# Residual blocks as whole rows: one DMA of 128x1024 in place of two of 128x512, and a new table of engine orders, in a two-layer hybrid decoder

## The chip, the core and the metric

The kernel runs on one core of a Trainium2 chip. The metric is the device time of one execution in microseconds (us), taken as the median of several. The core has a matmul engine (PE, with its weight loads PEld), a vector engine (DVE), an activation engine (ACT), GpSimd (POOL), and SyncE (SP), which issues every DMA of this kernel in one queue, in order.

## What is computed

Two decoder layers over x of 1024 tokens by 1024 features, all in float32. Cut to what matters here:

```python
for l in range(DEPTH):                      # 2
    proj = rmsnorm(x, attn_norm[l]) @ w_in[l]
    ... # four mixers: latent attention, gated convolution, pooling, sliding-window attention
    mixed = group_norm(stack(y_a, y_b, y_c, y_d)) * mix_norm[l]
    x = x + mixed @ w_o[l]                  # the residual add of this change
    gate, up = split(rmsnorm(x, ffn_norm[l]) @ w_gate_up[l])
    x = x + (silu(gate) * up) @ w_down[l]
return rmsnorm(x, final_norm)
```

## The kernel before, in words

Everything is kept transposed: a block is 128 features by 1024 tokens, there are 8 blocks d, and a block has two halves t of 512 tokens. Float32 products are made of three matmuls (`mm3`, L294) on numbers split in two parts: ACT rounds (`CAST`, L305 for data, L237 for weights), DVE subtracts (L306, L238). So every operand that PE reads has passed ACT and then DVE.

On-chip memory for blocks is a pool of 47 slots of 128x1024 (`Slots`), given out first in, first out while the program is written; a slot serves as a pair (128x1024) or as two halves. A DMA into a slot waits until the last reader of what was there before is done.

The stage of this change is the latent attention of a layer, steps n = 0 to 7, each one head and one half of the queries: scores (L1223 to L1225), softmax on DVE and ACT (L1231 to L1261), then, one step later, `mix_values`: PE transposes the probabilities (L1277), ACT and DVE split them (L305, L306), PE multiplies them with the values (L1289, into `ps_pv`), and L1304 and L1305 take the result away. Between these steps `out_some` issues the output projection in 16 pieces (`out_part`, d = 0 to 7, t = 1 then 0), each 18 matmuls into `ps_mm` with the groups b, c, d of `mixed`; group a is added later in `out_last`. L1327 adds a piece to its half of the residual x. That half comes from memory by `fetch_x` (L1343). The first three blocks (`NSP`) go back to memory as "mixed blocks" (`xp`, L1329) and are read again in `out_last` (L1397). The weights of a piece (`w_o`, L228) are loaded and split one block ahead. At the end of the stage the weights `w_oa` (L281) and the first weights of the feed-forward part (`w_gu`, L1435) follow.

The order in which each engine runs its instructions is not that of the program. `order_engines` collects the instructions in steps, gives each a place (its rank in the program plus an entry of the table `MOVES` for its group), and `arrange` walks through them with a table of durations: when an engine is free, it takes the ready step with the lowest place. The result is written out as a fixed order per engine, SP's DMA queue too. So both a new slot assignment and a new `MOVES` change the order on all engines, in stretches that the edited lines don't touch as well.

Of the kernel before, what the change touches and what calls it, by code (L numbers as in the profile page):

```python
# [22 lines left out]
HT = 512  # L23
NK = D // P
# [10 lines left out]
HALVES = (1, 0)  # L35
OUT_PARTS = tuple((d, t) for d in range(NK) for t in HALVES)
# [7 lines left out]
NSP = 3  # L44
# [78 lines left out]
def trunk_kernel(ctx: ExitStack, tc: tile.TileContext, ins, out):  # L123
    nc = tc.nc
    act, dve, pe, pool, sp = nc.scalar, nc.vector, nc.tensor, nc.gpsimd, nc.sync
# [254 lines left out]
    x_in = ins["xT"]  # L380
# [195 lines left out]
    for l in range(L):  # L576
# [735 lines left out]
        def out_part(d, t):  # L1312
            if t == HALVES[0]:
                out_w[:] = take()
                ahead()
            w = out_w
            s = residual.pop(0)
            if len(parts):
                fetch_x()
            p = ps("mm")  # L1320
            terms = []
            for k in (4, 5, 2, 3, 0, 1):
                hl = mixed["bcd"[k // 2], k % 2, t]
                ks = slice(k * P, (k + 1) * P)
                terms.append((w[0][:, ks], w[1][:, ks], R.ap(hl[0]), R.ap(hl[1])))
            mm3(p, terms)
            dve.tensor_tensor(out=F.ap(s), in0=F.ap(s), in1=p, op=ALU.add)  # L1327
            if d < NSP:
                sp.dma_start(xp[d][:, t * HT : (t + 1) * HT], F.ap(s))  # L1329
                F.free(s)  # L1330
            else:
                x[d][t] = s

        parts = deque(OUT_PARTS)
        coming = deque(OUT_PARTS)
        residual, out_w = [], []

        def fetch_x():
            if coming:
                d, t = coming.popleft()  # L1340
                s = F.half()
                src = x_in[d] if l == 0 else xs[d]
                sp.dma_start(F.ap(s), src[:, t * HT : (t + 1) * HT])  # L1343
                residual.append(s)
# [145 lines left out]
        for n, (h, t) in enumerate(steps):  # L1490
# [8 lines left out]
            if n == 0:  # L1499
# [13 lines left out]
                fetch_x()  # L1513
# [625 lines left out]
def arrange(steps, rank=lambda v: v.rank):  # L2139
# [380 lines left out]
```

## Time and profile before

| | |
|---|---|
| median of 3 runs | 2036.31 us (2035.26 to 2036.7) |
| the profiled execution | 2037.59 us, span of its instructions 2035.7 us |
| PE, PEld, DVE, ACT, POOL busy | 99%, 82%, 81%, 50%, 10% |
| DMA | 320.21 MB, q1 (SP's) 45.9% of 16 engines' span |
| residual loads L1343 | 32 of 256 KB, mixed blocks out L1329 12 and back L1397 12, of 256 KB |

PE is busy almost all the time, and busy time of PE is not a measure of what could be won, since its matmuls overlap. What can be won or lost is in the stretches where PE stands still, and these are found by the idle time in front of its instructions. The span has two such stretches by nature: the start, until the first blocks are loaded and split, and the end, where the last normalization and stores follow the last matmul. A row of a timeline gives start and duration, the engine, the line, and in brackets the idle time before it with what ended it.

### The profile page before, as it was taken

How to read it: one execution, taken by the hardware profiler on the slowest of the kernel's cores; microseconds unless marked ns; L12 is line 12 of the kernel's file. 1: busy time of each engine (PE TensorE's matmuls, PEld its weight loads, DVE VectorE, ACT ScalarE, POOL GpSimd, SP SyncE). 2: the span in 40 equal slices, each digit the busy share in tenths (PEclk: the TensorE clock that was granted, in tenths of full speed). 3: DMA queues.
4: the chain of work that ended last, by engine and by line, in shares of the span. 5: the costliest groups of instructions: out<-in, count | busy, mean ns of one | idle time of the engine just before them, and what ended most of it. 6: DMA issues, size and time to landing. Idle time of an engine off the chain costs nothing.

```text
span 2035.7 us, 26489 instructions
## 1 busy us (share of the span) xinstructions
PE 2015.7 (99%) x9378; PEld 1669.5 (82%) x9378; DVE 1646.4 (81%) x2793; ACT 1027.6 (50%) x1803; POOL 212.7 (10%) x212
## 2 busy tenths in 40 slices
PE   9999999999999999999999999999999999999998
PEld 8887888778888888888888878887888888888887
DVE  8889988998888888755778998989977787886555
ACT  7447666653333435433545676668433233355342
POOL 0000000013213213000000000000232212220000
PEclk9999999999999999999999999999999999999999
DMA  5101222346566667875455113241554454497652
GB/s 184 55 27 36 75 95 99 126 141 220 210 221 223 217 231 256 305 243 176 147 176 168 38 37 98 73 139 66 195 183 150 150 184 146 152 323 264 200 173 90
DMA packets 166949, 320.21 MB, mean 157 GB/s; under 512 B 13600, under 2 KB 85408, under 8 KB 166816
## 3 DMA queue, kind: packets, MB, share of 16 engines
q1 hardware_dynamic: 166816, 318.51, 45.9%
q8 instruction: 74, 1.21, 0.2%
q14 instruction: 59, 0.48, 0.1%
HBM read 220.41 MB, written 98.04 MB: 156 GB/s over the span
## 4 chain that ended last, share of the span: by engine, by line
PE 90%; DVE 5%; ACT 2%; DMA 2%; issue 1%; SPq 0%; DVEq 0%; ACTq 0%
PE ps_mm L294 34%; PE ps_s L294 28%; PE ps_t L294 11%; PE ps_pv L294 8%; PE ps_pv L1289 2%; PE ps_t L1277 1%; PE ps_s L1223 1%; PE ps_s L1225 1%; PE ps_s L1224 1%; DVE u L306 1%; PE ps_mm L1109 1%; PE ps_pv L814 1%; PE ps_s L753 1%; PE ps_t L802 1%; DVE u L309 1%
## 5 line engine op out<-in xcount | busy, mean ns | idle before, releaser
L294 PE MATMUL ps_mm<-u,u 128*128 128x512 f32 (+1 forms) x3402 | 852.3, 388 | 1.8 <-ACT u L305 0.8
L294 PEld LDWEIGHTS ps_mm<-u,u 128*128 128x128 f32 x3402 | 623.9, 188 | 128.2 <-issue 2.9
L294 PE MATMUL ps_s<-u,u 128*128 128x512 f32 x2628 | 645.8, 389 | 0.0
L294 PEld LDWEIGHTS ps_s<-u,u 128*128 128x128 f32 x2628 | 492.6, 188 | 103.6 <-ACT tn L458 1.0
L306 DVE TENSOR_TENSOR u<-u,u 128x1024 fp32r<-128x1024 f32 (+2 forms) x400 | 413.1, 1050 | 170.1 <-ACT u L305 123.2
L305 ACT CAST u<-u 128x1024 fp32r<-128x1024 f32 (+2 forms) x400 | 343.3, 881 | 407.8 <-PE ps_s L294 88.6
L294 PE MATMUL ps_t<-u,u 128*128 128x512 f32 (+1 forms) x1142 | 283.6, 377 | 0.9 <-DVE u L1408 0.6
L172 POOL TENSOR_TENSOR u<-u 128x256 f32<-128x256 f32 x176 | 205.9, 1171 | 748.7 <-DMA u<-in_w_dn 395.2
L294 PEld LDWEIGHTS ps_t<-u,u 128*128 128x128 f32 x1142 | 209.1, 188 | 41.7 <-DVE u L1408 1.1
L294 PE MATMUL ps_pv<-u,u 128*128 128x512 f32 x696 | 175.6, 390 | 0.2 <-ACT tn L458 0.2
L294 PEld LDWEIGHTS ps_pv<-u,u 128*128 128x128 f32 x696 | 130.4, 188 | 27.9 <-ACT tn L458 0.6
L1605 ACT ACTIVATE tp<-tp 128x512 f32<-128x512 f32 x84 | 53.1, 632 | 124.2 <-DVE tp L372 124.2
L1286 POOL MEMSET u<- 128x128 f32 x32 | 6.5, 231 | 857.0 <-DVE sm L1255 404.9
L305 ACT CAST u<-ps_t 128x512 fp32r<-128x512 f32 (+4 forms) x136 | 64.6, 507 | 60.8 <-PE ps_t L1277 32.9
L308 ACT ACTIVATE u<-u,par 128x512 fp32r<-128x512 f32 x100 | 69.5, 717 | 44.6 <-DVE u L372 14.9
L306 DVE TENSOR_TENSOR u<-ps_t,u 128x512 fp32r<-128x512 f32 (+4 forms) x136 | 76.3, 584 | 13.9 <-ACT u L305 13.1
L309 DVE SCALAR_TENSOR_TENSOR u<-u,par,u 128x512 fp32r<-128x512 f32 x100 | 73.2, 749 | 7.2 <-ACT u L308 7.0
L1606 DVE TENSOR_TENSOR tp<-tp,u 128x512 f32<-128x512 f32 x84 | 62.7, 747 | 13.4 <-ACT tp L1605 12.6
L458 ACT COPY tn<-ps_s 128x512 f32<-128x512 f32 x66 | 38.5, 583 | 67.1 <-PE ps_s L294 67.0
L340 ACT ACTIVATE tn<-u 128x512 f32<-128x512 f32 (+1 forms) x92 | 51.9, 592 | 38.2 <-DVE u L1883 35.3
L372 DVE TENSOR_TENSOR tp<-tp,u 128x512 f32<-128x512 f32 x80 | 60.6, 757 | 1.2
L1289 PE MATMUL ps_pv<-u,u 128*128 128x512 f32 (+2 forms) x184 | 51.9, 356 | 2.3 <-ACT u L305 2.3
(222 smaller groups left out, 2172.9 us busy)
## 6 DMA issues: line engine op xcount, KB each, us to landing
u<-in_w_gu SPq DMA_DIRECT2D x88, 512.0 KB, 3.8
ad<-u SPq DMA_DIRECT2D x154, 256.0 KB, 3.1
u<-ad SPq DMA_DIRECT2D x70, 512.0 KB, 5.0
u<-in_w_dn SPq DMA_DIRECT2D x68, 512.0 KB, 4.8
qd<-u SPq DMA_DIRECT2D x44, 512.0 KB, 3.0
u<-qd SPq DMA_DIRECT2D x32, 512.0 KB, 4.7
u<-in_w_in SPq DMA_DIRECT2D x29, 512.0 KB, 3.5
u<-ws SPq DMA_DIRECT2D x28, 512.0 KB, 3.5
```

What stands on the lines that cost most here:

```text
L172: pool.tensor_tensor(out=o, in0=o, in1=u, op=ALU.add)
L294: pe.matmul(o, w, r, start=start and k == 0 and i == 0, stop=stop and k == n - 1 and i == 2, skip_group_check=again,)
L305: act.copy(hi, f)
L306: dve.tensor_tensor(out=lo, in0=f, in1=rd(hi), op=ALU.subtract)
L308: act.activation(hi, f, AF.Copy, scale=gain)
L309: dve.scalar_tensor_tensor(out=lo, in0=f, scalar=gain, in1=rd(hi), op0=ALU.mult, op1=ALU.subtract)
L340: act.activation(q, f, AF.Square)
L372: dve.tensor_tensor(out=o, in0=a, in1=b, op=ALU.mult)
L458: act.copy(o, p)
L1289: pe.matmul(py[:, c0:], v_of(j, h), R.ap(s)[:, c0:], start=j == 0 and n == 0, stop=j == nj - 1 and n == 1,)
L1605: last_silu = act.activation(g, g, AF.Silu)
L1606: dve.tensor_tensor(out=g, in0=g, in1=r, op=ALU.mult)
```

## The change

`fetch_x` loads a block as one pair of 128x1024 by one DMA, when the first piece of the block before it begins; before, it loaded one half for each piece, two halves ahead. The blocks 0 to 2 go to `xp` as one DMA of 128x1024, after the second piece of the block; before, each half went out after its own piece and its half slot came free. Blocks 3 to 7 stay on chip in the same pair. `out_last` still reads `xp` in halves. That is 8 DMAs fewer for the residual and 3 fewer for `xp` in each layer, 22 in all; all other instructions are the same in kind and number. `MOVES` is another table, of about the same length.

```diff
@@ out_part
             w = out_w
+            if t == HALVES[0]:
+                fetch_x()
             s = residual.pop(0)
-            if len(parts):
-                fetch_x()
@@
             dve.tensor_tensor(out=F.ap(s), in0=F.ap(s), in1=p, op=ALU.add)
-            if d < NSP:
-                sp.dma_start(xp[d][:, t * HT : (t + 1) * HT], F.ap(s))
-                F.free(s)
-            else:
+            if d >= NSP:
                 x[d][t] = s
+            elif t == HALVES[1]:
+                i = s - t
+                sp.dma_start(xp[d], F.ap2(i))
+                F.free_pair(i)
 
-        coming = deque(OUT_PARTS)
+        coming = deque(range(NK))
@@ fetch_x
-                d, t = coming.popleft()
-                s = F.half()
-                src = x_in[d] if l == 0 else xs[d]
-                sp.dma_start(F.ap(s), src[:, t * HT : (t + 1) * HT])
-                residual.append(s)
+                d = coming.popleft()
+                s = F.pair()
+                sp.dma_start(F.ap2(s), x_in[d] if l == 0 else xs[d])
+                residual.extend(s + t for t in HALVES)
@@ after step 0
                 fetch_x()
-                fetch_x()
@@ MOVES
-    3: -950, 4: -948, 5: -885, 6: -594, 7: -545, 8: -946, 14: -632, 15: -897, 16: -459, 18:
+    3: -1110, 4: -1104, 5: -984, 7: -776, 8: -1105, 14: -914, 15: -964, 16: -307, 18: -279, 20:
```

What the new table and slots do to the order is shown at three places. The first is on ACT, in layer 0, late in the attention, where the weights of the last `w_o` block are split (L237; its slot is u40 before, u10 now). Before, it stood here:

```order
L305 CAST u32_2203<-ps_t_3520 128x512
L305 CAST u19_2227<-ps_t_3529 128x512
L1304 COPY tn_3413<-ps_pv_3336 64x512
L237 CAST u21_3440<-u40_3438 128x768
L305 CAST u32_2203<-ps_t_3538 128x512
L305 CAST u19_2227<-ps_t_3547 128x512
L285 CAST u2_3467<-u16_3465 128x1024
L1245 ACTIVATE u9_3477,sm2_3479<-ps_s_3481,sm1_3480 128x128
L285 CAST u30_3473<-u24_3471 128x1024
```

And now, in the same engine, with `ps_t_3529` being what was `ps_t_3538`:

```order
L1304 COPY tn_3407<-ps_pv_3330 64x512
L1245 ACTIVATE u4_504,sm2_3470<-ps_s_3472,sm1_3471 128x128
L305 CAST u32_2203<-ps_t_3511 128x512
L305 CAST u19_2227<-ps_t_3520 128x512
L1245 ACTIVATE u33_2070,sm2_3480<-ps_s_3482,sm1_3481 128x256
L1245 ACTIVATE u4_504,sm2_3490<-ps_s_3492,sm1_3491 128x384
L237 CAST u45_3432<-u10_3430 128x768
L1245 ACTIVATE u0_503,sm2_3500<-ps_s_3502,sm1_3501 128x512
L305 CAST u24_3661<-u5_3631 128x1024
L305 CAST u32_2203<-ps_t_3529 128x512
L305 CAST u19_2227<-ps_t_3538 128x512
L285 CAST u20_3460<-u28_3458 128x1024
```

Four exponentials of the next scores (L1245) and a split of feed-forward weights (L305 of 128x1024) now stand ahead of the split that PE's next product needs.

The second place is on ACT in layer 1, where the first queries of the latent attention are split (`te` to `u`, L305) for the first scores; `ps_mm` holds the values (L1155), `ps_t` a normalization (L362 to L364). Before:

```order
L237 CAST u40_11056<-u43_11054 128x768
L1155 CAST u29_11152<-ps_mm_11153 128x4x64
L362 ACTIVATE tn_11198<-ps_t_11192 128x512
L237 CAST vhi_11242<-vraw_11240 128x256
L1155 CAST u43_11140<-ps_mm_11141 128x4x64
L363 ACTIVATE tn_11198<-tn_11198 128x512
L1155 CAST u29_11152<-ps_mm_11153 128x4x64
L305 CAST u32_11131<-te_11129 128x512
```

And now:

```order
L237 CAST u22_11047<-u26_11045 128x768
L237 CAST vhi_11233<-vraw_11231 128x256
L305 CAST u41_11184<-u18_10998 128x512
L1155 CAST u4_11143<-ps_mm_11144 128x4x64
L305 CAST u32_11122<-te_11120 128x512
L1155 CAST u26_11131<-ps_mm_11132 128x4x64
L1155 CAST u4_11143<-ps_mm_11144 128x4x64
L1155 CAST u26_11131<-ps_mm_11132 128x4x64
```

Two copies of values and two steps of the normalization moved from ahead of the query split to behind it.

The third place is on PE in layer 1, where the chain of transposes (L1277) and products with the values (L1289) of one head and half begins; `ps_mm` is a projection. Before:

```order
L294 MATMUL ps_mm_11623<-u25_11226,u32_11429 128x512 x2
L294 MATMUL ps_mm_11623<-u25_11226,u17_11430 128x512
L294 MATMUL ps_mm_11623<-u18_11229,u32_11429 128x512 x2
L294 MATMUL ps_mm_11623<-u18_11229,u17_11430 128x512
L1277 MATMUL ps_t_11515<-cst_76,u2_11259 128x128 x2
L1277 MATMUL ps_t_11515<-cst_76,u42_11298 128x128 x2
```

And now, where `ps_mm_11583` is the output piece that came before `ps_mm_11623`, which is `ps_mm_11612` in the new numbers:

```order
L294 MATMUL ps_mm_11583<-u17_10694,u1_11370 128x512
L294 MATMUL ps_mm_11583<-u12_11223,u9_11369 128x512 x2
L294 MATMUL ps_mm_11583<-u12_11223,u1_11370 128x512
L1277 MATMUL ps_t_11504<-cst_76,u30_11249 128x128 x2
L1277 MATMUL ps_t_11504<-cst_76,u42_11288 128x128 x2
L1277 MATMUL ps_t_11514<-cst_76,u30_11249 128x128 x2
L1277 MATMUL ps_t_11514<-cst_76,u42_11288 128x128 x2
L294 MATMUL ps_mm_11583<-u34_11226,u9_11369 128x512 x2
L294 MATMUL ps_mm_11583<-u34_11226,u1_11370 128x512
L1289 MATMUL ps_pv_11503<-u3_11509,u26_11131 128x512
```

The chain now begins before the output piece ahead of it is finished: the 18 matmuls of one more output piece and 6 of the next queries (24 of 128x512) that stood ahead of it have moved behind its begin. At the same chain in layer 0 it is 22 matmuls of output pieces.

136 rows, old and new, of the table MOVES are left out of this document.

## The prediction

> **What bounds the kernel now.** I read the page first for shares and for the chain that ended last, then PE's waits, then windows, then single stretches of the timeline.
>
> ```profile
> PE 2015.7 (99%) x9378; PEld 1669.5 (82%) x9378; DVE 1646.4 (81%) x2793; ACT 1027.6 (50%) x1803; POOL 212.7 (10%) x212
> PE 90%; DVE 5%; ACT 2%; DMA 2%; issue 1%; SPq 0%; DVEq 0%; ACTq 0%
> 812.21 22.44 PE ps_s L294 x99
> ```
>
> PE is the bound: it holds 90% of the chain, and where nothing disturbs it one 128x512 matmul follows another after 22.44 / 99 = 0.227 us. The change leaves the number of matmuls as it is, so it can only move the time in which PE stands still. How much there is, the windows tell (the columns are length, then busy time of PE, PEld, DVE, ACT, POOL, the granted clock PEclk, DMA):
>
> ```profile
> 0.00:50.00 50.00, 48.64 (x218) 40.84 (x219) 39.96 (x65) 37.20 (x60) 0.20 (x4) 1.00 0.52 187
> 200.00:250.00 50.00, 48.21 (x234) 40.09 (x233) 48.98 (x108) 32.97 (x72) 0.34 (x2) 1.00 0.22 75
> 300.00:350.00 50.00, 47.74 (x249) 40.26 (x248) 42.98 (x107) 34.51 (x80) 1.46 (x6) 0.97 0.29 95
> 1200.00:1250.00 50.00, 47.73 (x233) 39.24 (x232) 49.19 (x106) 32.56 (x70) 0.35 (x2) 1.00 0.22 71
> 0.00:2000.00 2000.00, 1989.06 (x9165) 1643.73 (x9166) 1626.54 (x2749) 1018.67 (x1783) 212.66 (x212) 1.00 0.46 158
> 2000.00:2035.70 35.70, 26.63 (x216) 25.77 (x214) 19.89 (x44) 8.93 (x21) 0.00 (x0) 0.93 0.33 118
> ```
>
> The last 35.7 us hold 9.1 us of idle PE, the final normalization and stores; the order of the last stores is nearly the same after the change, and I count nothing there. Before 2000 us PE is idle for 10.94 us, 1.36 of them at the start. The 9.6 us left lie mostly in three windows of the attention (1.8, 2.3 and 2.3 us). The waits of PE (total, times, longest; 13 rows in all) name them:
>
> ```profile
> PE ps_s L1223 <- ACT u L305: 3.2, 2, 1.9
> PE ps_pv L1289 <- ACT u L305: 2.3, 1, 2.3
> ...
> PE ps_pv L294 <- ACT tn L458: 0.2, 1, 0.2
> ```
>
> **The transfers themselves.** 22 DMAs fall away. What one costs SP, and how long transfers of either size take to land:
>
> ```profile
> 341.02 0.33 SPq L1343 DMA_DIRECT2D u<-in_xT  x1
> u<-in_xT SPq DMA_DIRECT2D x32, 256.0 KB, 3.5
> u<-xs SPq DMA_DIRECT2D x20, 256.0 KB, 2.8
> u<-in_w_in SPq DMA_DIRECT2D x29, 512.0 KB, 3.5
> u<-in_w_oa SPq DMA_DIRECT2D x4, 512.0 KB, 5.4
> ```
>
> SP saves 22 x 0.33 = 7.3 us of issuing, which is worth nothing: SP has 0% of the chain. A whole block may land up to 5.4 - 2.8 = 2.6 us later than a half did, or no later (3.5 against 3.5). It is asked for one block ahead, that is 36 matmuls or 8.2 us of PE, which hides either; without that cover DVE's add L1327 would be late by up to 2.6 us at each of 16 blocks, 42 us, and a bank of `ps_mm` with it. The added wait is that of a whole slot: behind a load that waits for one stand, on SP, the next `w_o`, `w_uq` and `w_oa`, and for these ACT and then PE. I take 0, since 8.2 us of cover is three times the worst delay, and keep the other end out of the range for the same reason. A pair for `xp` also leaves its slot one piece (18 x 0.227 = 4.1 us) later; with 47 slots I count nothing. What remains is the new order, and it decides.
>
> **Term A, the late weights in layer 0.** The chain, then ACT, then PE, at 326 to 334 us:
>
> ```profile
> 326.25 6.34 DMA u<-in_w_o
> 328.39 0.58 ACT L1304 COPY tn<-ps_pv 64x512 f32<-64x512 f32 x1
> 332.67 0.83 ACT L237 CAST u<-u 128x768 fp32r<-128x768 f32 x1 [3.70 <-DMA u<-in_w_o]
> 333.53 0.59 ACT L305 CAST u<-ps_t 128x512 fp32r<-128x512 f32 x1
> 334.17 0.54 PE L1289 MATMUL ps_pv<-u,u 128*128 128x512 f32 x1 [2.26 <-ACT u L305]
> 334.40:338.00 3.60, 3.60 (x14) 3.11 (x14) 3.60 (x8) 3.14 (x7) 0.00 (x0) 0.53 0.33 133
> ```
>
> ACT stands 3.70 us at the split of the last `w_o` block; the split PE needs is queued behind it. And the stall costs twice: in the 3.6 us after it the granted clock is 0.53, which takes (1 - 0.53) x 3.6 = 1.7 us more. In layer 1 the longest stall (1.92 us, below) is followed by no such drop: its window has 1.00. After the change four exponentials and one split stand ahead of PE's split on ACT. Their rows in the present order:
>
> ```profile
> 335.44 0.38 ACT L1245 ACTIVATE u<-ps_s,sm 128x128 f32<-128x128 f32 x1
> 339.30 1.05 ACT L305 CAST u<-u 128x1024 fp32r<-128x1024 f32 x1
> 344.75 0.48 ACT L1245 ACTIVATE u<-ps_s,sm 128x256 f32<-128x256 f32 x1
> 345.73 0.57 ACT L1245 ACTIVATE u<-ps_s,sm 128x384 f32<-128x384 f32 x1
> 346.29 0.69 ACT L1245 ACTIVATE u<-ps_s,sm 128x512 f32<-128x512 f32 x1
> ```
>
> Together 3.2 us, which fit into the 3.70 us of idle time, so the split comes 0.5 us earlier if the weights are there. `w_o` still waits for the same reader of its slot, but only one `w_oa` stands beside it now in place of two and of two residual halves. The row of `w_o` on the page has 3.0 us to land, so 326.25 + 3.0 = 329.3, ahead of need; with 6.34 again ACT would wait to 332.6 as now. On PE the scores of those exponentials (three of 128x512, two of 128x256: 3 x 0.227 + 2 x 0.12 = 0.9 us) move ahead of the stalled product. 2.26 - 0.5 - 0.9 leaves 0.9; I take 1.0, that is -1.3 us, and with the stall so short the clock stays up, -1.7 us. The ends are 0 and -4.0.
>
> A rule of the Trainium skill speaks against the second half: "TensorE: Matmul & The Clock Gate", "What's actually happening", has the clock fall only after an idle window of some 3.4 us, in windows that run free. The trace differs, with the drop after 2.26 us of idle; by the rule the 1.7 us would belong to something else and the sum would be 1.7 us higher.
>
> **Terms B, C, D, first queries and a later split.** Rows of layer 1 (ACT, then PE) and two of PE in the layers 0 and 1:
>
> ```profile
> 1224.61 0.60 ACT L362 ACTIVATE tn<-ps_t 128x512 f32<-128x512 f32 x1
> 1225.10 0.41 ACT L237 CAST vhi<-vraw 128x256 fp32r<-128x256 f32 x1
> 1225.39 0.39 ACT L1155 CAST u<-ps_mm 128x256 fp32r<-128x256 f32 x1
> 1225.66 0.65 ACT L363 ACTIVATE tn<-tn 128x512 f32<-128x512 f32 x1
> 1226.19 0.38 ACT L1155 CAST u<-ps_mm 128x256 fp32r<-128x256 f32 x1
> 1226.44 0.65 ACT L305 CAST u<-te 128x512 fp32r<-128x512 f32 x1
> 1227.14 0.50 PE L1223 MATMUL ps_s<-u,u 128*128 128x512 f32 x1 [1.92 <-ACT u L305]
> 225.31 0.39 PE L294 MATMUL ps_mm<-vhi,u 128*128 128x256 f32 x1 [0.55 <-DVE u L1156]
> 1435.37 1.88 PE L294 MATMUL ps_mm<-u,u 128*128 128x512 f32 x7 [0.33 <-DVE u L306]
> ```
>
> B: L362, one L1155, L363 and the second L1155 leave the place ahead of the query split; from start to start that is 0.49 + 0.27 + 0.53 + 0.25 = 1.5 us on ACT. The queries' own matmuls are issued ahead of the values now, so DVE's `te` is early enough. PE loses one 0.23 us matmul of cover. -1.3 us, with ends 0 (DVE is 98% busy in this window and `te` can still be late) and -1.9. C: in layer 0 the order puts all value matmuls ahead of the first scores, so the 0.55 us wait behind them has no place left, while the wait for the scores themselves keeps its size: ACT's four added instructions there eat the added cover. -0.6, ends -1.8 and +0.6. D: five DVE instructions fewer stand ahead of the split at 1435 us: -0.3, ends 0 and -0.3.
>
> **Term E, what the new order spends.** At the chain of transposes in both layers the matmuls that stood ahead move behind its begin: 24 x 0.227 = 5.4 us in layer 1, 22 x 0.227 = 5.0 us in layer 0. PE reaches the chain that much earlier, but the splits are made by ACT and DVE. In layer 1 another 1.0 us of scores moved behind, ACT has 1.1 us less ahead of the first split, and the split was 0.6 us early: short by 5.4 + 1.0 - 1.1 - 0.6 = 4.7 us. In layer 0 scores moved ahead (0.9 us), four transposes behind (0.4 us), ACT has 1.0 us more ahead and the slack is 0.3 us: 5.0 - 0.9 + 0.4 + 1.0 - 0.3 = 5.2 us. What the engines have in hand there, and how often DVE's split waits for ACT's:
>
> ```profile
> 250.00:262.00 12.00, 12.00 (x68) 10.36 (x67) 7.61 (x21) 5.09 (x12) 0.69 (x4) 1.00 0.37 122
> 1255.00:1275.00 20.00, 20.00 (x109) 16.84 (x108) 15.98 (x43) 11.12 (x27) 0.70 (x4) 1.00 0.33 106
> DVE u L306 <- ACT u L305: 138.5, 120, 5.7
> ```
>
> DVE is idle for 4.4 us and 4.0 us. If all of it can be used, 0.8 and 0.7 us are left, +1.5 us; if none, +9.9 us; if the matmuls just fill the chain, 0. I take +1.5, since the order has other matmuls between the products in both chains.
>
> **The sum:** -1.3 - 1.7 - 1.3 - 0.6 - 0.3 + 1.5 = -3.7 us. The profiled execution took 2037.59 us (1.9 around its span), which makes 2033.9; it lay 1.3 us above the median of the runs, 2036.31, so I carry the difference over: **2032.6 us**. That is 0.18% below; 0.2% (4.1 us) is about what a measurement of this kernel can tell from no change, so the bounds of "same" are 2032.2 and 2040.4.
>
> **The rivals.**
> *More is won:* DVE's idle time at the two chains is filled with work that now stands in windows where it is 98% busy, and the waits there shrink as well. At most all 9.6 us of idle PE and the 1.7 us go: 2036.3 - 11.3 = 2025.0. For it speaks that DVE, not ACT, is near full in 200:250 and 1200:1250; against it that most of these waits are for the next link of one chain (PE, ACT, DVE, PE), which other work can cover but not shorten. Midway between the sum and that floor: 2028.
> *Nothing is won:* the order moves waits without lessening them, and fewer DMAs change nothing off the chain: 2036. For it: the weights of term A wait for the same reader as before.
> *Slower, the transposes starve:* at the two chains DVE's idle time is waiting for ACT and PE, not spare, so the full 9.9 us show (+8.4 on the sum), in two stalls of 5 us, longer than the 2.26 us that halved the clock, so 2 x 1.7 us more: 2032.6 + 8.4 + 3.4 = 2044.4. It decides from the point where less than about a third of the 8.4 us can be used (2040.4). For it: DVE's split waits for ACT's 120 times, 138.5 us in all; against it: PE was busy throughout in both windows.
> *The clock of the rule above:* 2032.6 + 1.7 = 2034.3.
>
> **How the numbers follow.** The forecast (2029 to 2036) gets 0.42, of which 0.20 below 2032.2; more is won 0.17; nothing is won 0.10; starving transposes 0.27; the other clock 0.04. Faster 0.20 + 0.17 = 0.37, same 0.22 + 0.10 + 0.04 = 0.36, slower 0.27. Cases of both signs hold weight, so the range goes from the floor, 2025, to just over the slower rival, 2045; the likeliest case's own is 2029 to 2036.
>
> **What would show it.** A: PE's wait for ACT L305 at an L1289 near 334 us below 1.5 us, and no window with PEclk near 0.5 there. B: the wait at the first L1223 of layer 1 below 1 us. C: no wait for L1156 near 225 us. E: idle PE in 250:270 and 1250:1275, 100% busy now; over 3 us in either speaks for the slower rival. Wrong altogether would be a residual load that PE or DVE waits for (L1327 on `in_xT` or `xs`), or a wait of SP for a whole slot with `w_o` behind it.

## The result, and the profile after

| | before | after |
|---|---|---|
| median, same chip | 2035.62 us (2034.74 to 2039.32, 18 runs) | 2032.84 us (2031.56 to 2034.04, 18 runs) |
| ratio, 95% interval | | 0.9984 (0.9978 to 0.9990) |
| the profiled execution | 2037.59 us, span 2035.7 | 2032.88 us, span 2031.1 |

The change is worth 2.8 us (2.0 to 4.5), 0.16%, where 2032.6 us had been predicted. First the page of the changed kernel, its busy row and the shares of the chain that ended last:

```profile
PE 2014.0 (99%) x9378; PEld 1669.4 (82%) x9378; DVE 1644.2 (81%) x2793; ACT 1030.7 (51%) x1803; POOL 210.7 (10%) x212
PE 93%; DVE 3%; ACT 2%; DMA 1%; issue 1%; SPq 0%; DVEq 0%; ACTq 0%
```

As many matmuls as before, and DVE's share of the chain is down from 5% to 3%. The windows of the changed kernel (length, busy PE, PEld, DVE, ACT, POOL, PEclk, DMA) say where:

```profile
0.00:50.00 50.00, 47.68 (x213) 39.88 (x214) 39.28 (x64) 37.17 (x60) 0.20 (x4) 1.00 0.51 187
200.00:250.00 50.00, 48.21 (x237) 39.98 (x236) 49.74 (x116) 33.54 (x77) 0.35 (x2) 1.00 0.22 76
300.00:350.00 50.00, 50.00 (x269) 41.62 (x268) 45.52 (x110) 35.95 (x82) 1.62 (x8) 1.00 0.31 106
1200.00:1250.00 50.00, 48.88 (x235) 39.75 (x234) 49.87 (x113) 34.28 (x76) 0.35 (x2) 1.00 0.22 77
0.00:2000.00 2000.00, 1992.45 (x9207) 1648.70 (x9208) 1629.91 (x2759) 1023.83 (x1787) 210.70 (x212) 1.00 0.46 158
2000.00:2031.10 31.10, 21.54 (x173) 20.68 (x171) 14.25 (x35) 6.87 (x16) 0.00 (x0) 0.89 0.32 114
```

Idle PE before 2000 us went from 10.94 to 2000 - 1992.45 = 7.55 us, behind it from 9.07 to 31.10 - 21.54 = 9.56: 2.9 us less in all. The half clock at 334 us is gone (PEclk 1.00 in 300:350, 0.97 before): 1.7 us. Together 4.6 us, which is the difference of the two spans, 2035.7 - 2031.1. Window 300:350 gives the most, 2.26 us of idle PE and the clock; 1200:1250 gives 1.15; 200:250 is the same to the digit; 0:50 is 0.96 worse.

What PE still waits for in the changed kernel (total, times, longest), 7.9 us in 8 rows where 13 rows stood:

```profile
PE ps_mm L294 <- DVE u L1156: 2.6, 2, 1.8
PE ps_mm L294 <- ACT u L237: 1.3, 1, 1.3
...
PE ps_mm L294 <- ACT u L305: 1.0, 1, 1.0
PE ps_t L294 <- ACT u L305: 0.8, 1, 0.8
...
PE ps_s L1223 <- ACT u L305: 0.3, 1, 0.3
```

The wait at L1289 is gone, that at L1223 is down from 3.2 to 0.3 us, and L1156, DVE's eviction of the values, now leads. Behind the start, three stalls of PE stand out in the timeline of the changed kernel:

```profile
223.69 0.36 PE L294 MATMUL ps_mm<-vhi,u 128*128 128x256 f32 x1 [1.79 <-DVE u L1156]
...
1226.17 0.70 PE L294 MATMUL ps_mm<-u,vhi 128*128 128x512 f32 x2 [0.85 <-DVE u L1156]
...
1419.97 0.73 PE L294 MATMUL ps_mm<-u,u 128*128 128x512 f32 x2 [1.03 <-ACT u L305]
```

Now term A. SP's queue in the kernel before (start, then the time that SP spent on issuing):

```profile
324.97 0.80 SPq L1343 DMA_DIRECT2D u<-in_xT  x2
326.25 0.33 SPq L228 DMA_DIRECT2D u<-in_w_o  x1
326.63 2.56 SPq L281 DMA_DIRECT2D u<-in_w_oa  x2
```

and in the changed kernel:

```profile
321.52 0.33 SPq L1343 DMA_DIRECT2D u<-in_xT  x1
321.94 0.38 SPq L281 DMA_DIRECT2D u<-in_w_oa  x1
326.72 0.33 SPq L228 DMA_DIRECT2D u<-in_w_o  x1
332.54 0.33 SPq L281 DMA_DIRECT2D u<-in_w_oa  x1
```

and, on ACT, the split of `w_o` and the next split for PE's products with the values:

```profile
330.60 0.86 ACT L237 CAST u<-u 128x768 fp32r<-128x768 f32 x1
...
333.74 1.08 ACT L305 CAST u<-ps_t 128x512 fp32r<-128x512 f32 x2 [0.66 <-PE ps_t L1277]
```

`w_o` is asked for no sooner than before (326.25), but nothing stands near it: the row of x and the first `w_oa` went 5 us ahead, the second `w_oa` follows 6 us later. The DMA view of 318 to 340 us (size, median us to landing), before:

```profile
u<-in_w_o SPq DMA_DIRECT2D x1, 384.0 KB, 6.3
```

and after:

```profile
u<-in_w_o SPq DMA_DIRECT2D x1, 384.0 KB, 2.9
```

So L237 finds its weights there and has no idle time in front of it, and at the next split ACT waits for PE's transposes, not PE for ACT.

### The profile page after: what moved, and what is told of

It is laid out like the page before. It is cut to its first block, busy times and chain, and to the rows that moved or that the text cites. A ratio compares the mean times of both kernels' runs of the same rounds, so it can differ in the third digit from the quotient of the medians.

```text
span 2031.1 us, 26457 instructions
## 1 busy us (share of the span) xinstructions
PE 2014.0 (99%) x9378; PEld 1669.4 (82%) x9378; DVE 1644.2 (81%) x2793; ACT 1030.7 (51%) x1803; POOL 210.7 (10%) x212
## 4 chain that ended last, share of the span: by engine, by line
PE 93%; DVE 3%; ACT 2%; DMA 1%; issue 1%; SPq 0%; DVEq 0%; ACTq 0%
PE ps_mm L294 37%; PE ps_s L294 28%; PE ps_t L294 11%; PE ps_pv L294 8%; PE ps_pv L1289 2%; PE ps_t L1277 2%; PE ps_s L1223 1%; PE ps_s L1224 1%; PE ps_s L1225 1%; PE ps_pv L814 1%; PE ps_s L753 1%; PE ps_mm L1109 1%; PE ps_t L802 1%; DVE u L346 1%; DVE u L306 1%
## 5 line engine op out<-in xcount | busy, mean ns | idle before, releaser
L305 ACT CAST u<-u 128x1024 fp32r<-128x1024 f32 (+2 forms) x400 | 344.3, 883 | 412.1 <-PE ps_s L294 82.1
L306 DVE TENSOR_TENSOR u<-u,u 128x1024 fp32r<-128x1024 f32 (+2 forms) x400 | 412.7, 1049 | 165.2 <-ACT u L305 127.3
L294 PE MATMUL ps_t<-u,u 128*128 128x512 f32 (+1 forms) x1142 | 275.1, 378 | 1.2 <-ACT u L305 0.8
L1604 ACT ACTIVATE tp<-tp 128x512 f32<-128x512 f32 x84 | 53.3, 634 | 117.1 <-DVE tp L372 116.8
L305 ACT CAST u<-ps_t 128x512 fp32r<-128x512 f32 (+4 forms) x136 | 64.9, 507 | 58.7 <-PE ps_t L1277 34.1
L306 DVE TENSOR_TENSOR u<-ps_t,u 128x512 fp32r<-128x512 f32 (+4 forms) x136 | 77.0, 584 | 13.6 <-ACT u L305 12.7
L1289 PE MATMUL ps_pv<-u,u 128*128 128x512 f32 (+2 forms) x184 | 54.4, 358 | 0.0
```

Source lines behind the costliest of these rows:

```text
L294: pe.matmul(o, w, r, start=start and k == 0 and i == 0, stop=stop and k == n - 1 and i == 2, skip_group_check=again,)
L305: act.copy(hi, f)
L306: dve.tensor_tensor(out=lo, in0=f, in1=rd(hi), op=ALU.subtract)
L1289: pe.matmul(py[:, c0:], v_of(j, h), R.ap(s)[:, c0:], start=j == 0 and n == 0, stop=j == nj - 1 and n == 1,)
L1604: last_silu = act.activation(g, g, AF.Silu)
```

## The experiments

Every experiment was compared with the kernel before on the same chip; that had medians of 2035.7 to 2036.8 us there.

### Transfers, slots or order

`split_rows_new_order`: the changed kernel, each row moved as two halves, with its slots and, by a table, its order kept.

```diff
-                sp.dma_start(F.ap2(s), x_in[d] if l == 0 else xs[d])
+                for t in HALVES:
+                    sp.dma_start(F.ap(s + t), src[:, t * HT : (t + 1) * HT])
...
-                sp.dma_start(xp[d], F.ap2(i))
+                for t in HALVES:
+                    sp.dma_start(xp[d][:, t * HT : (t + 1) * HT], F.ap(i + t))
```

> The changed kernel with its slots and its order, but each row of the residual and of xp moved as two halves, one right behind the other: 22 more DMAs, 7.3 us more of issuing on SP. Theory 'order' and the prediction (transfers are worth 0): 2032.8 us within 0.6. Rival 'size of the transfers': 2035.6 us, with SP or the landing of a half in front of a wait of PE or DVE.

Measured: 2033.19 us, ratio 0.9987 (0.9978 to 0.9996), against 0.9984 for the changed kernel. 22 DMAs more cost 0.35 us by the medians (2033.19 against 2032.84), well inside the intervals; within what these can tell, the number and size of the transfers are worth 0, as predicted.

`new_rows_old_order` and `old_rows_new_order`: a table with one place for each step, taken from the other kernel, in place of `MOVES`.

```diff
 def places(steps):
...
-        v.place = v.rank + MOVES.get(groups[k], 0)
+    for v, n in zip(steps, PLACES_OF_THE_OTHER):
+        v.place = v.rank + n
```

> The changed code with its whole-row transfers and its slots, while every instruction takes the place in the order that its counterpart has in the kernel before (a row's load that of the first of the two halves). Theory 'order' (the 2.8 us came from the new places, not from the transfers): 2035.6 us, and at about 330 us PE waits over 1.5 us for ACT L305 at an L1289, since w_o is again asked for just ahead of two w_oa. Rival 'transfers' (fewer, larger DMAs and other slots bring the gain whatever the order): 2032.8 us and no such wait.

> The code before, with two half transfers a block and its own slots, while every instruction takes the place that its counterpart has in the changed kernel (both halves that of the row). Theory 'order': 2032.8 us, without the wait for w_o near 330 us. Rival 'transfers': 2035.6 us. A result between the two would say that the order is worth part of it and the slots the rest.

Measured: 2045.67 us, ratio 1.0047 (1.0035 to 1.0060), and 2046.93 us, ratio 1.0054 (1.0042 to 1.0067). Both theories fall: either half of the change alone is 9 to 10 us slower than the kernel before. In both the 2.26 us stall at L1289 near 330 us is gone, so term A goes with either half; what is lost lies elsewhere. `new_rows_old_order`, PE, and the window behind it:

```profile
420.45 2.56 PE L294 MATMUL ps_s<-u,u 128*128 128x512 f32 x5 [2.35 <-ACT u L305]
424.34 1.22 PE L294 MATMUL ps_t<-u,u 128*128 128x512 f32 x2 [1.33 <-DVE u L306]
```

```profile
420.00:430.00 10.00, 8.21 (x18) 5.91 (x19) 8.63 (x14) 7.75 (x12) 0.00 (x0) 0.51 0.15 50
```

Behind the stall the clock is halved for 10 us. `old_rows_new_order` has 2.86 and 1.57 us at the same place, and half clock. Between 50 and 2000 us PE is idle for 12.78 and 14.30 us (9.58 before), and four and two steps of 3.4 us run at half clock (one before). Why is argued, not shown: a place is a priority, not a time, so with other slots other steps are ready when an engine comes free, and the stretch behind the attention, where ACT works all the time from 412 to 425 us in `new_rows_old_order`, falls out of step. What is shown is that "the order" can't be moved alone: with the other kernel's slots either table loses, and only the pair brings the 2.8 us.

### Why `w_o` was late, and what the late split cost

`old_split_behind`: the kernel before, one step moved on ACT (and its partner on DVE).

```diff
-L237 CAST u21_3440<-u40_3438 128x768
 L305 CAST u32_2203<-ps_t_3538 128x512
 L305 CAST u19_2227<-ps_t_3547 128x512
+L237 CAST u21_3440<-u40_3438 128x768
```

> The kernel before with one step moved: ACT's split of the late w_o block (L237) stands behind the two L305 that PE waits for, and DVE's L238 behind the two L306. The matmul that needs w_o itself stands 3 matmuls further on, so PE's stall at 334 us should shrink from 2.3 to about 1.2 us. Theory 'the half clock follows the length of the stall': no stretch with a clock near 0.5 after it, together -1.1 - 1.7 = -2.8, 2032.8 us. Rival 'the half clock has another cause' (the hour, the work there): the stretch of 3.6 us at 0.53 stays, 2034.5 us.

Measured: 2035.34 us, ratio 0.9995 (0.9986 to 1.0004). Timelines of ACT and PE and a window, `old_split_behind`:

```profile
331.38 1.07 ACT L305 CAST u<-ps_t 128x512 fp32r<-128x512 f32 x2 [1.40 <-PE ps_pv L1289]
...
333.66 0.83 ACT L237 CAST u<-u 128x768 fp32r<-128x768 f32 x1 [1.20 <-DMA u<-in_w_o]
```

```profile
334.54 0.50 PE L294 MATMUL ps_mm<-u,u 128*128 128x512 f32 x1 [0.92 <-ACT u L237]
```

```profile
334.00:338.00 4.00, 3.10 (x15) 2.17 (x16) 2.95 (x4) 3.56 (x7) 0.00 (x0) 1.00 0.68 270
```

The stall shrinks from 2.26 to 0.92 us and the clock stays at 1.00 (0.53 before): in this trace the half clock is gone with the long stall. The time alone could not tell the two theories apart: 1.0 us by the ratio, with an interval of 1.8 us to each side, is nearer to the rival's 1.1 us than to the theory's 2.8. The stalls made on purpose, below, settle it.

`new_loads_beside`: the changed kernel with four loads more behind `w_o`.

```diff
+    def weights_beside(*args):
+        for n in range(4):
+            sp.dma_start(xd[n], ins["w_gu"][0, n, 0])
+        return weights(*args)
```

> The changed kernel with four more transfers of 512 KB (memory to memory, read by nothing) right behind the w_o load that was late in layer 0 before; every other instruction in its old order. Theory 'w_o was late because transfers asked for just behind it share the DMA engines': it lands over 5.5 us after its issue in place of 2.9, ACT waits over 1 us at its split L237, PE stalls by 1 to 3 us near 330 us, and behind a stall over 2.2 us the clock is near 0.5 for some 3.5 us: 2034 to 2037.5 us. Rival 'it was late because it was asked for late (the reader of its slot)': it still lands in about 3 us, 2032.8 us.

Measured: 2036.35 us (2031.88 to 2038.74), ratio 0.9998 (0.9989 to 1.0007). The DMA view of 318 to 340 us:

```profile
xd<-in_w_gu SPq DMA_DIRECT2D x4, 512.0 KB, 6.8
...
u<-in_w_o SPq DMA_DIRECT2D x1, 384.0 KB, 3.1
```

`w_o` lands in 3.1 us: transfers behind it alone don't delay it, and the theory falls in that form. It is the `w_oa` behind them that comes late; ACT waits 2.11 us for it, PE 1.3. So the two neighbours were taken apart in the kernel before:

`old_halves_behind` and `old_oa_behind`, SP's queue:

```diff
+DMA u_3438<-in_w_o 128x768
 DMA u_3416<-in_xT 128x512 x2
-DMA u_3438<-in_w_o 128x768
 DMA u_3465<-in_w_oa 128x1024
 DMA u_3471<-in_w_oa 128x1024
```

```diff
 DMA u_3438<-in_w_o 128x768
+DMA u_3675<-in_w_gu 128x1024
+DMA u_3676<-in_w_gu 128x1024
 DMA u_3465<-in_w_oa 128x1024
 DMA u_3471<-in_w_oa 128x1024
-DMA u_3675<-in_w_gu 128x1024
-DMA u_3676<-in_w_gu 128x1024
```

> The kernel before with one step moved on SP: the load of w_o that was late in layer 0 is asked for ahead of the two residual halves, not behind them; the two w_oa stay right behind. Theory 'the halves ahead of it made w_o late': it lands in 3 to 4 us in place of 6.3, ACT's 3.70 us at L237 go, PE's stall at 334 us falls below 0.5 us and no half clock follows: 2035.7 - 2.3 - 1.7 = 2031.7 us. Rival 'the w_oa behind share the engines with it': it still takes over 5 us, the stall stays near 2 us, 2035.7 us.

> The kernel before with the two w_oa asked for behind the next two w_gu, so that only the halves stand close to w_o. Theory 'the halves ahead of it': w_o still takes over 5 us to land. Rival 'the w_oa behind': it lands in 3 to 4 us, the 2.3 us stall of PE goes, and a later one takes its place where ACT waits for w_oa at L285.

Measured: 2036.09 us, ratio 1.0000 (0.9991 to 1.0009), and 2037.95 us, from one execution. DMA view, ACT and PE of `old_halves_behind`:

```profile
u<-in_w_o SPq DMA_DIRECT2D x1, 384.0 KB, 3.2
```

```profile
334.00 1.04 ACT L285 CAST u<-u 128x1024 fp32r<-128x1024 f32 x1 [2.36 <-DMA u<-in_w_oa]
```

```profile
335.45 0.50 PE L1223 MATMUL ps_s<-u,u 128*128 128x512 f32 x1 [1.47 <-ACT u L1245]
```

and DMA view and PE of `old_oa_behind`:

```profile
u<-in_w_o SPq DMA_DIRECT2D x1, 384.0 KB, 3.9
```

```profile
338.13 0.50 PE L1223 MATMUL ps_s<-u,u 128*128 128x512 f32 x1 [3.26 <-ACT u L1245]
```

Each theory is half right: `w_o` is late only with the halves just ahead of it and the `w_oa` just behind; with either away it lands in 3 to 4 us. And neither wins anything, because the same bytes are then late one block further on: `w_oa` comes in place of `w_o`, ACT waits for it in front of the next exponentials, and PE with it. In these 6 us 2 x 256 + 384 + 2 x 512 + 2 x 512 KB are asked for. What the changed kernel does differently is to ask for a third of it (a row and a `w_oa`) 5 us sooner and for the rest, but `w_o`, some 6 us later.

### The clock behind a stall

`stall_ladder` and `stall_phase`: the changed kernel with made stalls on PE.

```diff
+    for _, cols in LADDER:
+        for n in cols:
+            pool.memset(spare[:, :n], 0.0)
...
+        tc.add_manual_dep(chain[0], pe[k].ins[-1].name, sync, reason="idle")
+        tc.add_manual_dep(pe[k + 1].ins[0], chain[-1].name, sync, reason="idle")
```

> The changed kernel with 12 stalls of PE made on purpose, 26 us apart from 840 us on, where PE, ACT and DVE have no other stall: a matmul waits for memsets on the idle POOL of a spare tile that nothing reads, in lengths for 0.8, 1.2, 1.5, 1.8, 2.0, 2.2, 2.5, 2.8, 3.2, 3.6, 4.2 and 5.0 us. Theory 'the half clock follows a stall, from a length between 1.9 and 2.3 us': the stalls up to about 2.0 leave 1.00, from 2.5 on a stretch of about 3.4 us at 0.5 follows each. Rival 'only a stall of about 3.4 us or more drops the clock': the stretches begin at 3.6. Rival 'the drop has nothing to do with a stall': none.

The memsets were shorter than planned, so the stalls ran from 0.28 to 2.56 us; the time, 2055.42 us, is mostly the stalls. Up to 1.56 us none was followed by half clock, from 1.82 us each was. Two of its PE rows:

```profile
1065.28 1.89 PE L295 MATMUL ps_mm<-u,u 128*128 128x512 f32 x7 [1.56 <-POOL spare L1972]
...
1093.48 0.96 PE L295 MATMUL ps_mm<-u,u 128*128 128x512 f32 x2 [1.82 <-POOL spare L1972]
```

But in the kernel before 1.92 us at 1227 us had no such effect. The starts of all half-clock stretches of one trace lie on a grid of 3.413 us, which led to the second run.

> The changed kernel with 14 made stalls from 840 us on, 20 us apart, of about 2.05 and 2.75 us in turn. In the runs so far the half clock began on a grid of 3.413 us in every trace, and followed when PE had stood still for 1.99 us or more inside one step of that grid, never for 1.85 or less. Theory 'fixed windows': a stall of 2.75 us that a grid line cuts so that each part is under 1.85 is followed by no half clock (about 3 in 10 of them), and one of 2.05 us only if it lies wholly inside a step (about 4 in 10). Rival 'length alone, from about 2.4 us': all of 2.75 are followed by it, none of 2.05.

Measured: 2089.51 us. (The idle time in a row's bracket is 0.16 us less than the lengths of the expectation, which count from where the next matmul was due.) Of seven stalls of 1.82 to 1.88 us four were followed by half clock, the four that lie wholly inside one step (of the others one is cut in the middle, and two, 1.88 us long like those four, lose 0.03 and 0.07 us to the next step); of seven of 2.58 to 2.67 us all were, since the grid happened to leave 2.2 us or more of each in one step. A stall that a grid line (850.55 us) cuts into 0.99 and 0.83 us, and one that lies in the step from 894.92 to 898.33 us, PE of `stall_phase`:

```profile
851.37 8.69 PE L295 MATMUL ps_t<-u,u 128*128 128x512 f32 x37 [1.82 <-POOL spare L1972]
...
898.15 15.06 PE L295 MATMUL ps_mm<-u,u 128*128 128x512 f32 x58 [1.88 <-POOL spare L1972]
```

and the steps behind them (PEclk is the third number from the end):

```profile
850.55:853.96 3.41, 2.59 (x11) 2.17 (x12) 1.61 (x3) 1.80 (x3) 0.65 (x3) 1.00 0.21 31
853.96:857.37 3.41, 3.41 (x16) 2.82 (x16) 1.07 (x2) 0.00 (x0) 0.00 (x0) 1.00 0.80 269
898.33:901.74 3.41, 3.41 (x9) 2.64 (x10) 0.00 (x0) 0.00 (x0) 0.00 (x0) 0.50 0.00 0
```

Nearly the same length, without half clock and with it; the 1.82 us of the ladder, inside a step, had it too. Length alone does not decide, and the rival, which has none of the shorter stalls followed by it, falls. The case of a long stall cut into two short parts did not come up here, but it stands in `old_rows_new_order`: 2.11 us at 1435.8 us, cut into 0.78 and 1.33, no half clock. In the traces of all 13 kernels there are 43 stalls of over 1.35 us. By the idle time inside one step: 1.88 us or more, 20 of 20 followed by half clock; 1.77 to 1.85 us, 4 of 8; 1.69 us or less, 1 of 15, and that one, 0.94 us, stands inside a half-clock stretch that an earlier stall of 2.86 us had begun. Inside such a stretch less is enough: in `new_rows_old_order` the steps from 420.17 and 423.58 us, with 0.86 and 0.75 us of idle PE, were each followed by another at half clock.

The same shows without made stalls. The wait of 1.92 us at the first L1223 of layer 1 stands in four traces: in `old_halves_behind` it lies inside one step, and half clock follows; in the kernel before, `old_oa_behind` and `old_split_behind` a grid line leaves at most 1.77, 1.49 and 1.30 us of it in one step, and none does.

### What is left

`new_near`: neighbours exchanged at the four largest stalls of the changed kernel; of ACT at 221 us:

```diff
-L1155 CAST u_2203<-ps_mm 128x4x64
-L1155 CAST u_2215<-ps_mm 128x4x64
-L362 ACTIVATE tn<-ps_t 128x512
-L1155 CAST u_2203<-ps_mm 128x4x64
-L363 ACTIVATE tn<-tn 128x512
-L1155 CAST u_2215<-ps_mm 128x4x64
+L1155 CAST u_2203<-ps_mm 128x4x64 x2
+L1155 CAST u_2215<-ps_mm 128x4x64 x2
+L362 ACTIVATE tn<-ps_t 128x512
+L363 ACTIVATE tn<-tn 128x512
```

> The changed kernel with a few neighbours exchanged at the four largest stalls of PE that are left in it: at the value products of both layers all evictions L1155 and L1156 of a bank stand together (ahead of L362, L363, of a te and of a vlo), and at 416 and 1418 us ACT's split L305 of 128x1024 stands ahead of one or two L466/L467. Theory 'these stalls are the order of ACT and DVE within a few instructions': 2.06 shrinks by about 1.0, 1.02 by 0.85, 0.95 by up to 0.5, 1.19 by up to 0.8: 2029.7 to 2031 us. Rival 'DVE, 98% busy there, only passes the wait on': the same sum of stalls a few matmuls further on, 2032.8 us or more.

Measured: 2035.16 us, ratio 0.9998 (0.9989 to 1.0006). The rival holds; PE of `new_near`, where one stall of 1.79 us stood:

```profile
222.45 0.36 PE L294 MATMUL ps_mm<-vhi,u 128*128 128x256 f32 x1 [0.79 <-DVE u L1156]
224.24 0.36 PE L294 MATMUL ps_mm<-vhi,u 128*128 128x256 f32 x1 [0.84 <-DVE u L1156]
228.27 0.51 PE L355 MATMUL ps_t<-u,ones_r 128*128 128x512 f32 x1 [0.63 <-ACT u L305]
```

0.79 + 0.84 + 0.17 (a wait at 225.36) + 0.63 is more than 1.79. DVE is busy 49.74 of 50 us there in the changed kernel; what is put ahead makes something else late. Of the other three stalls 0.79 us shrank to 0.35, but 1.03 us became 1.54, and 0.85 became 0.27 with 1.09 us behind it.

`new_one_table`: one table load less on ACT in each layer.

```diff
+    for n in range(L):
+        TABLES.append(act.preload_act_table_set("natural_log_exp_and_others").ins)
...
+                if (table, v.table) == ("Silu", "Exp"):
+                    turns += 1
+                    if turns % 2:
+                        ins = [TABLES[turns // 2]] + ins
```

> The changed kernel with one table load of ACT fewer in each layer: ahead of the first L362 behind a Silu the table that serves both L362 and L363 is loaded, in place of one for L362 and one more, 2.4 us later, for L363 (1.28 us each). At 416 and 1418 us PE stalls 0.95 and 1.19 us for a split of ACT, which has no idle time from the first of these loads on. Theory 'these stalls are ACT's backlog': both go and nothing takes their place, 2032.8 - 2.1 = 2030.7 us, faster than both kernels. Rival 'DVE, next in the chain, is as late': a wait for DVE L306 of about the same size, 2032.8 us.

Measured: 2031.58 us (2029.83 to 2033.37), ratio 0.9978 (0.9969 to 0.9987). ACT of `new_one_table`, one load between L1604 and L363 in place of two, and the windows (1400:1450 had 48.97, 400:450 had 48.79 busy in the changed kernel):

```profile
409.91 1.28 ACT L1970 ACT_TABLE_LOAD   x1
411.21 0.60 ACT L362 ACTIVATE tn<-ps_pv 128x512 f32<-128x512 f32 x1
411.70 0.61 ACT L305 CAST u<-tp 128x512 fp32r<-128x512 f32 x1
412.21 0.63 ACT L363 ACTIVATE tn<-tn 128x512 f32<-128x512 f32 x1
```

```profile
400.00:450.00 50.00, 49.08 (x213) 39.35 (x212) 47.57 (x72) 30.83 (x46) 4.09 (x4) 1.00 0.41 134
1400.00:1450.00 50.00, 50.00 (x221) 41.13 (x220) 49.73 (x74) 31.35 (x47) 7.28 (x7) 1.00 0.42 143
```

In layer 1 the theory holds: the 1.03 us go and nothing takes their place. In layer 0 the wait for ACT goes, but waits for DVE's L306 (0.8 us in two) take most of it. 1.3 us in sum, in the trace and in the medians (2032.84 to 2031.58, each against the kernel before, at different times, with intervals of the ratio that overlap). It is the fastest version seen, faster than the kernel before beyond doubt; against the changed kernel the trace shows the gain and the times allow it.

## Why the prediction was right, step by step

**The transfers, 0:** right, by `split_rows_new_order`. What the text called "the new order, and it decides" was too simple: new places without the new slots lose 10 us.

**Term A, -1.3 and -1.7:** the largest term, and the right one. The landing (3.0 us forecast, 2.9 measured) and the clock came as written; the stall was to leave 1.0 us and left nothing. The text counted only 0.9 us of scores that move ahead of the stalled product, but on PE 13 matmuls into `ps_mm` now stand between the two groups of transposes, 5 before (8 x 0.227 = 1.8 us more), so that these groups begin 5.6 us apart (327.47 and 333.05 us) and not 2.3 (326.65 and 328.91), and ACT is ready ahead of the second. -2.3 - 1.7 = -4.0, the far end of its range. That the clock hung on the stall is shown by `stall_ladder` and `stall_phase`, and `old_split_behind` agrees. But -1.7 is the price in this one execution: it depends on where the grid lies. A stall of 2.26 us leaves 1.85 us or more in one step for (1.56 + 0.41) / 3.41 = 58% of the positions (3.41 - 1.85 = 1.56 and 2.26 - 1.85 = 0.41), one of 1.92 us for 48% (an estimate from the threshold above; in the four traces it was 1 of 4), so the kernel before pays about (0.58 + 0.48) x 1.7 = 1.8 us on average, not always 1.7 at 334 us; and the changed kernel pays too, behind its 1.79 us at 223 us: half clock followed this stall in 3 of the 7 traces that have it, some 0.7 us on average. By this estimate the clock's part of the gain is nearer 1.1 us. That accounts for 0.6 of the 1.8 us by which the profiled spans differ more (4.6 us) than the medians (2.8); the wait at 1119 us, below, may be another 0.8, and the rest stays open.

**Term B, -1.3:** the wait at the first L1223 of layer 1 fell from 1.92 to 0.27 us, as forecast. Not foreseen was the wait of 0.85 us for L1156 at 1226 us behind it. Net -0.8.

**Term C, -0.6:** wrong. The text has "the wait for the scores themselves keeps its size" and the 0.55 us behind them without a place. It went the other way round: the scores wait no more, and the value products wait 1.79 us for L1156, as much as both waits before (1.24 + 0.55). The step that failed counted what stood ahead of the scores on ACT and on PE, but not the evictions of the values on DVE, the engine that is full there; `new_near` shows that this wait is DVE's and can be moved, not removed, by such exchanges.

**Term D, -0.3:** the 0.33 us at 1435 us went, but 1.03 us came at 1420 us, from ACT, whose two table loads stand in front; `new_one_table` shows that.

**Term E, +1.5:** wrong in size, 0 measured. The windows of the changed kernel:

```profile
250.00:262.00 12.00, 12.00 (x65) 9.96 (x64) 9.40 (x20) 6.25 (x13) 0.72 (x4) 1.00 0.43 138
1255.00:1275.00 20.00, 20.00 (x108) 16.90 (x108) 15.18 (x37) 11.33 (x28) 0.35 (x2) 1.00 0.31 101
```

The step that failed is the shortage of 4.7 and 5.2 us, set against DVE's idle time: PE is busy throughout, and DVE did 1.8 us more in 250:262 (9.40, 7.61 before) and still has 2.6 us to spare. The order found other matmuls for the chain; the rival of starving transposes, 0.27, has nothing in the trace for it.

Two waits that no term named went as well: 0.79 us due to L306 at 1119 us and 0.65 us due to L1408 at 385 us; a third, 0.81 us at 425 us, returned as 0.79 us at 417. The wait at 1119 us stands in none of the traces of `old_split_behind`, `old_halves_behind` and `old_oa_behind`, which differ from the kernel before only near 330 us, so it may belong to that one execution and not to the order. The start cost 0.96 us more in this profile; in the experiments the start varies as much, whichever order they have (1.36 to 4.25 us of idle PE in the first 50 us, over all 13 traces).

In sum: the mechanism of the largest term was right; the time came out within 0.3 us because errors cancelled: A was worth 1 us more in this execution, C, D and B 2 us less, E 1.5 us less loss, and of the clock's gain only part shows in the median. The base was off as well: 2036.31 us, the median of three runs, against 2035.62 of 18. As a change -3.7 us were forecast and -2.8 measured, and the base hides 0.7 of the difference. That the time came out so near is luck.

## What to carry to other kernels

When a load is late, add up everything that is asked for in the microseconds around it: moving one request only made its neighbour late here, while in the changed kernel, where a third of it is asked for 5 us earlier, PE waits for none of it. On DVE, busy nearly all the time in that stretch, exchanging neighbours moved a wait and didn't remove it; taking work away (a table load on ACT) removed one in layer 1. An order table belongs to the slot assignment it was made with: here neither could be judged, or kept, without the other.

## What the runs showed of the hardware

The granted clock of TensorE is set in steps of 3.413 us on a grid that the kernel's start doesn't shift: in all 13 traces every half-clock stretch begins on it. A step in which PE stood still for about 1.85 us or more, 54% of it, is followed by one at half clock, 0.5 x 3.41 = 1.7 us lost; idle time on both sides of a grid line doesn't add up (2.11 us cut into 0.78 and 1.33: no half clock), and behind a step that is already at half clock 0.75 us was enough. So stalls of 1.79 and 1.92 us had this price in some executions and not in others, and a profile shows one draw. The Trainium skill, "TensorE: Matmul & The Clock Gate", section "What's actually happening", gives the same length of step, 3413 ns, and has it run free, and the traces agree; it has the clock fall after an idle window, and there they differ: the window need not be idle, 1.88 of 3.41 us were enough in 20 of 20 cases.

ACT loads a table for L362 and one more for L363 when the two follow a Silu, 1.28 us each (at 409.45 and 411.87 us in the changed kernel); asked for by name, one load serves both (`new_one_table`, 409.91 us).
